# Log-softmax over 50000 columns: stores issued by SyncE between the loads, loads issued three tiles ahead

## The chip, the cores and the metric

The kernel runs on one core of a Trainium2 chip. The metric is the device time of one execution in microseconds. Before the change the median of three runs is 7614.17 us (7613.93 to 7614.27).

## The reference

For each of 16 x 512 = 8192 rows of 50000 float32 numbers, the log of the softmax:

```python
max_x = np.max(x, axis=-1, keepdims=True)
shifted = x - max_x
log_sum_exp = np.log(np.sum(np.exp(shifted), axis=-1, keepdims=True))
return (shifted - log_sum_exp).astype(np.float32)
```

1638.4 MB are read and as many written.

## The kernel before

The 8192 rows are cut into 512 tiles of 16 rows. Each row is cut into 8 pieces of 6250 numbers, and each piece lies on a partition of its own, so that a tile is 128 partitions x 6250 floats, 25000 bytes per partition, 3125 KB in all. A tile lives in one of 8 buffers (`NBUF`, pool `data`) from its load to its store; the result is written in place.

What is done with tile t stands in three helpers.

- `load(t)`: one DMA from the input to a buffer, issued by SyncE (line 75).
- `front(t)`: VectorE takes the maximum of each partition (`pmax`, line 81). Four small VectorE steps bring the 8 partial maxima of a row together and spread the negated row maximum over its 8 partitions (`allmax` L84, `rowmax` L86, `spread` L91, `negmax` L96). ScalarE takes the exponential of both halves with that bias, with the sum of each half into `part` (L102). TensorE adds the 16 partial sums of each row with a matrix of ones (L108), and ScalarE takes the logarithm (`logsum`, L112).
- `back(t)`: VectorE subtracts maximum and logarithm in place (L117). Then ScalarE issues the store (L121).

The order on each engine is the order of the program, since the scheduler is off (`manual_schedule`); only the semaphores are put in by the framework. The main loop sets that order:

```python
    for t in range(AHEAD):
        load(t)
    for t in range(ntiles + 1):
        if t < ntiles:
            front(t)
        if t >= 1:
            back(t - 1)
        if t + AHEAD < ntiles:
            load(t + AHEAD)
```

So VectorE takes the maximum of tile t before it ends tile t-1, and ScalarE issues the store of tile t-1 behind the exponentials of tile t. SyncE issues loads alone. `AHEAD` is 7. The load of tile t+7 takes the buffer that tile t-1 leaves, and waits until the store of tile t-1 has landed. The DMAs that SyncE issues go into queue 1 of the profile, those that ScalarE issues into queue 10. Both are served by the same 16 DMA engines: each engine gets 8 partitions of every transfer, that is 8 packets of 25000 bytes, and a packet of 4 bytes that counts the semaphore up.

Of the kernel before, what the change touches and what calls it, by code (L numbers as in the profile page):

```python
# [1 line left out]

# [4 lines left out]


FP32 = mybir.dt.float32
ACT = mybir.ActivationFunctionType  # L10
ALU = mybir.AluOpType
AX = mybir.AxisListType.X

P = 128
SQ = 32

G = 8
R = P // G
EXP_C = 3125
NBUF = 8  # L20
AHEAD = 7


@with_exitstack
def kernel(
    ctx: ExitStack,
    tc: tile.TileContext,
    x: bass.AP,
    out: bass.AP,
):  # L30
    nc = tc.nc
    xf = x.flatten_outer_dims()
    of = out.flatten_outer_dims()
    N, V = xf.shape
    W = V // G
    assert N % R == 0 and V % G == 0 and W % EXP_C == 0
    ntiles = N // R
    nexp = W // EXP_C

    xt = xf.rearrange("(t r) (g w) -> t (r g) w", r=R, g=G)  # L40
    ot = of.rearrange("(t r) (g w) -> t (r g) w", r=R, g=G)

    data = ctx.enter_context(tc.tile_pool(name="data", bufs=NBUF))
    stats = ctx.enter_context(tc.tile_pool(name="stats", bufs=4))
    consts = ctx.enter_context(tc.tile_pool(name="consts", bufs=1))
    dump_pool = ctx.enter_context(
        tc.tile_pool(name="dump", bufs=1, space=bass.MemoryType.PSUM)
    )
    sum_pool = ctx.enter_context(
        tc.tile_pool(name="sums", bufs=1, space=bass.MemoryType.PSUM)  # L50
    )

    ctx.enter_context(tc.manual_schedule())


    ones = consts.tile([P, P], FP32)
    nc.gpsimd.memset(ones, 1.0)  # L57
    ones3 = ones.rearrange("p (r g) -> p r g", g=G)
    nc.gpsimd.affine_select(  # L59
        out=ones3, in_=ones3, pattern=[[-G, R], [0, G]], base=0,  # L60
        channel_multiplier=1, compare_op=ALU.is_ge, fill=0.0,
    )
    nc.gpsimd.affine_select(  # L63
        out=ones3, in_=ones3, pattern=[[G, R], [0, G]], base=G - 1,
        channel_multiplier=-1, compare_op=ALU.is_ge, fill=0.0,
    )
    nc.scalar.preload_act_table_set("natural_log_exp_and_others")  # L67

    tiles = {}
    shift = {}  # L70
    logs = {}

    def load(t):
        buf = data.tile([P, W], FP32, name="buf")
        nc.sync.dma_start(out=buf, in_=xt[t])
        tiles[t] = buf

    def front(t):
        buf = tiles[t]
        pmax = stats.tile([P, 1], FP32, name="pmax")  # L80
        nc.vector.reduce_max(out=pmax, in_=buf, axis=AX)  # L81

        allmax = stats.tile([P, SQ], FP32, name="allmax")
        nc.vector.transpose(out=allmax, in_=pmax.to_broadcast([P, SQ]))  # L84
        rowmax = stats.tile([P, SQ // G], FP32, name="rowmax")
        nc.vector.tensor_reduce(  # L86
            out=rowmax, in_=allmax.rearrange("p (r g) -> p r g", g=G),
            op=ALU.max, axis=AX, negate=True,
        )
        spread = stats.tile([P, SQ], FP32, name="spread")  # L90
        nc.vector.tensor_copy(  # L91
            out=spread.rearrange("p (r g) -> p r g", g=G),
            in_=rowmax[:, :, None].to_broadcast([P, SQ // G, G]),
        )
        negmax = stats.tile([P, SQ], FP32, name="negmax")
        nc.vector.transpose(out=negmax, in_=spread)  # L96
        shift[t] = negmax

        part = stats.tile([P, nexp], FP32, name="part")
        for j in range(nexp):  # L100
            dump = dump_pool.tile([P, EXP_C], FP32, name="dump")
            nc.scalar.activation(  # L102
                out=dump, in_=buf[:, j * EXP_C : (j + 1) * EXP_C], func=ACT.Exp,
                bias=negmax[:, 0:1], scale=1.0, accum_out=part[:, j : j + 1],
            )
        rowsum = sum_pool.tile([P, 1], FP32, name="rowsum")
        for j in range(nexp):
            nc.tensor.matmul(  # L108
                rowsum, ones, part[:, j : j + 1], start=j == 0, stop=j == nexp - 1
            )  # L110
        logsum = stats.tile([P, 1], FP32, name="logsum")
        nc.scalar.activation(out=logsum, in_=rowsum, func=ACT.Ln)  # L112
        logs[t] = logsum

    def back(t):
        buf = tiles.pop(t)
        nc.vector.tensor_scalar(  # L117
            out=buf, in0=buf, scalar1=shift.pop(t)[:, 0:1], scalar2=logs.pop(t),
            op0=ALU.add, op1=ALU.subtract,
        )  # L120
        nc.scalar.dma_start(out=ot[t], in_=buf)  # L121

    for t in range(AHEAD):
        load(t)
# [9 lines that stand above are left out]
# [1 line left out]
_INS = ['x']  # L135
_OUTS = [((16, 512, 50000), 'float32')]


# [23 lines left out]
```

## Time and profile before

| | |
|---|---|
| median of three runs | 7614.17 us |
| profiled execution, its own time | 7614.27 us |
| its span | 7612.6 us |
| granted TensorE clock | 1.000 |
| VectorE busy | 5567.2 us, 73% |
| ScalarE busy | 3153.1 us, 41% |
| maximum L81, one instruction | 6664 ns |
| exponential L102, one instruction (two per tile) | 2869 ns |
| subtraction L117, one instruction | 3496 ns |
| idle time of VectorE before L81 | 1953.7 us |
| mean rate of the DMAs | 431 GB/s |

The span is the time from the first to the last instruction of the profiled execution; some 1.7 us of its time lie outside it. Busy shares are shares of the span. A group of instructions is named by line, engine, operation and tiles; behind it stand the busy time, the mean of one, the idle time of the engine just before the instructions of that group and what ended most of it. The DMA part of the page gives the packets, bytes and times by queue. Under that level the trace has a record of every packet, with queue, start, duration and bytes, but without the number of its engine.

### The profile page before, as it was taken

To read this page: it belongs to the slowest core of one execution; us is meant where nothing else is said; L and a number is where in the kernel's file an instruction comes from. 1 tells how busy PE (TensorE), PEld (TensorE's weight loads), DVE (VectorE), ACT (ScalarE), POOL (GpSimd) and SP (SyncE) were. 2 spreads that over 40 slices of the span, in tenths; PEclk is the share of its full clock that TensorE was granted. 3 is DMA by queue.
4 is the path that set the end of the run, shared out by engine and by line. 5 is a ranking of instruction groups with operands and counts; after the bars stand their busy time and mean duration, and the time that the engine had idled before them with its cause. 6 is when DMAs were issued, how large, how long until landed. Compare 5 with 4: busy or idle time off the path is not lost.

```text
span 7612.6 us, 12833 instructions
## 1 busy us (share of the span) xinstructions
PE 600.6 (8%) x2048; PEld 513.2 (7%) x2048; DVE 5567.2 (73%) x3072; ACT 3153.1 (41%) x2561; POOL 1.2 (0%) x7
## 2 busy tenths in 40 slices
PE   0000000000000000000000000000000000000000
PEld 0000000000000000000000000000000000000000
DVE  7777777777777777777777777777777777777776
ACT  4444444444444444444444444444444444444443
POOL 0000000000000000000000000000000000000000
DMA  9999999999999999999999999999999999999998
GB/s 425 433 432 432 432 432 432 432 432 432 432 432 432 432 432 432 432 432 432 432 432 432 432 432 432 432 432 432 432 432 432 432 432 432 431 432 432 432 432 380
DMA packets 147540, 3277.68 MB, mean 431 GB/s; under 512 B 16384, under 2 KB 16384, under 8 KB 16384
## 3 DMA queue, kind: packets, MB, share of 16 engines
q1 hardware_dynamic: 73728, 1638.43, 50.0%
q10 hardware_dynamic: 73728, 1638.43, 50.0%
q14 instruction: 68, 0.56, 0.0%
q8 instruction: 16, 0.26, 0.0%
HBM read 1638.40 MB, written 1638.40 MB: 430 GB/s over the span
## 4 chain that ended last, share of the span: by engine, by line
DVE 73%; another core or an unknown queue 25%; issue 1%; DMA 0%; ACT 0%; PE 0%; ACTq 0%
DVE pmax L81 45%; DVE buf L117 23%; DVE allmax L84 1%; DVE rowmax L86 1%; DVE spread L91 1%; DVE negmax L96 0%; DMA buf<-in_x_dram 0%; ACT dump L102 0%; PE rowsum L108 0%; ACT logsum L112 0%; ACTq L102 0%
## 5 line engine op out<-in xcount | busy, mean ns | idle before, releaser
L81 DVE TENSOR_REDUCE pmax<-buf 128x1 f32<-128x6250 f32 x512 | 3411.8, 6664 | 1953.7 <-DMA buf<-in_x_dram 1953.7
L102 ACT ACTIVATE dump<-buf,negmax 128x3125 f32<-128x3125 f32 x1024 | 2938.1, 2869 | 4092.9 <-DVE negmax L96 4029.5
L117 DVE TENSOR_SCALAR buf<-buf,negmax,logsum 128x6250 f32<-128x6250 f32 x512 | 1789.7, 3496 | 4.5 <-ACT logsum L112 3.6
L108 PE MATMUL rowsum<-part,ones 128*128 128x1 f32 x2048 | 600.6, 363 | 6991.7 <-ACT dump L102 6991.7
L108 PEld LDWEIGHTS rowsum<-part,ones 128*128 128x128 f32 x2048 | 513.2, 311 | 7079.0 <-ACT dump L102 7057.2
L112 ACT ACTIVATE logsum<-rowsum 128x1 f32<-128x1 f32 x512 | 87.6, 171 | 345.8 <-PE rowsum L108 345.8
L102 ACT ACTIVATION_READ_ACCUMULATOR dump<-buf,negmax 128x1 f32 x1024 | 191.1, 187 | 0.0
L96 DVE STREAM_TRANSPOSE negmax<-spread 128x32 f32<-128x32 f32 x512 | 108.2, 211 | 17.7
L84 DVE STREAM_TRANSPOSE allmax<-pmax 128x32 f32<-128x32 f32 x512 | 108.3, 211 | 17.4
L86 DVE TENSOR_REDUCE rowmax<-allmax 128x4 f32<-128x32 f32 x512 | 95.3, 186 | 17.7
L91 DVE COPY spread<-rowmax 128x32 f32<-128x32 f32 x512 | 92.9, 181 | 17.8
L67 ACT ACT_TABLE_LOAD x1 | 1.3, 1283 | 0.8 <-PEq L146 0.8
L59 POOL TENSOR_SCALAR_AFFINE_SELECT ones<-ones 128x128 f32<-128x128 f32 x1 | 0.4, 403 | 0.1
L63 POOL TENSOR_SCALAR_AFFINE_SELECT ones<-ones 128x128 f32<-128x128 f32 x1 | 0.4, 397 | 0.1
L57 POOL MEMSET ones<- 128x128 f32 x1 | 0.2, 204 | 0.3 <-POOLq L146 0.3
L146 POOL MEMSET const-bfloat16-1.0<- 128x1 bf16 x1 | 0.1, 101 | 0.0
L146 POOL MEMSET const-uint8-127<- 128x1 uint8 x1 | 0.1, 101 | 0.0
L146 POOL MEMSET const-float32-0.0<- 128x1 f32 x1 | 0.1, 98 | 0.3 <-issue 0.3
L146 POOL MEMSET const-float32-1.0<- 128x1 f32 x1 | 0.1, 98 | 0.0
## 6 DMA issues: line engine op xcount, KB each, us to landing
buf<-in_x_dram SPq DMA_DIRECT2D x512, 3125.0 KB, 51.9
out_dram<-buf ACTq DMA_DIRECT2D x512, 3125.0 KB, 37.5
```

The source lines that it names most:

```text
L59: nc.gpsimd.affine_select(out=ones3, in_=ones3, pattern=[[-G, R], [0, G]], base=0, channel_multiplier=1, compare_op=ALU.is_ge, fill=0.0,)
L63: nc.gpsimd.affine_select(out=ones3, in_=ones3, pattern=[[G, R], [0, G]], base=G - 1, channel_multiplier=-1, compare_op=ALU.is_ge, fill=0.0,)
L67: nc.scalar.preload_act_table_set("natural_log_exp_and_others")
L81: nc.vector.reduce_max(out=pmax, in_=buf, axis=AX)
L84: nc.vector.transpose(out=allmax, in_=pmax.to_broadcast([P, SQ]))
L86: nc.vector.tensor_reduce(out=rowmax, in_=allmax.rearrange("p (r g) -> p r g", g=G), op=ALU.max, axis=AX, negate=True,)
L91: nc.vector.tensor_copy(out=spread.rearrange("p (r g) -> p r g", g=G), in_=rowmax[:, :, None].to_broadcast([P, SQ // G, G]),)
L96: nc.vector.transpose(out=negmax, in_=spread)
L102: nc.scalar.activation(out=dump, in_=buf[:, j * EXP_C : (j + 1) * EXP_C], func=ACT.Exp, bias=negmax[:, 0:1], scale=1.0, accum_out=part[:, ...
L108: nc.tensor.matmul(rowsum, ones, part[:, j : j + 1], start=j == 0, stop=j == nexp - 1)
L112: nc.scalar.activation(out=logsum, in_=rowsum, func=ACT.Ln)
L117: nc.vector.tensor_scalar(out=buf, in0=buf, scalar1=shift.pop(t)[:, 0:1], scalar2=logs.pop(t), op0=ALU.add, op1=ALU.subtract,)
```

## The change

The store of a tile is issued by SyncE instead of ScalarE, and `AHEAD` is 3 instead of 7. Everything else stays, the 8 buffers and the main loop too. SyncE's order is then load 0, 1, 2, 3, store 0, load 4, store 1, load 5, and so on: store t-1, then load t+3. A store waits for L117 of its tile, and the load behind it in SyncE's order waits with it. All transfers go into the queue of SyncE.

```diff
 NBUF = 8
-AHEAD = 7
+AHEAD = 3
...
             op0=ALU.add, op1=ALU.subtract,
         )
-        nc.scalar.dma_start(out=ot[t], in_=buf)
+        nc.sync.dma_start(out=ot[t], in_=buf)
 
     for t in range(AHEAD):
         load(t)
```

## The prediction

> **What bounds the kernel now.** I read the page first (busy shares, slices, DMA queues), then the waits of VectorE and of SyncE's queue between 1000 and 7000 us, then the timeline of one tile, and last the DMA packets one by one.
>
> The page's engine line and its DMA lines:
>
> ```profile
> PE 600.6 (8%) x2048; PEld 513.2 (7%) x2048; DVE 5567.2 (73%) x3072; ACT 3153.1 (41%) x2561; POOL 1.2 (0%) x7
> ...
> DMA packets 147540, 3277.68 MB, mean 431 GB/s; under 512 B 16384, under 2 KB 16384, under 8 KB 16384
> ...
> q1 hardware_dynamic: 73728, 1638.43, 50.0%
> q10 hardware_dynamic: 73728, 1638.43, 50.0%
> ```
>
> No compute engine is over 73%. Queue 1 (loads, from SP) and queue 10 (stores, from ACT) fill 50.0% each of sixteen DMA engines' span: together the DMA engines have no free time. The waits in the steady stretch, VectorE's and SyncE's (us in total, times, longest):
>
> ```profile
> DVE pmax L81 <- DMA buf<-in_x_dram: 1556.5, 405, 4.6
> ```
>
> ```profile
> SPq L75 <- DMA out_dram<-buf: 5861.2, 405, 14.9
> ```
>
> VectorE waits for the load of every tile. SyncE stands 5861 of 6000 us before a load, waiting for the store that frees its buffer. One tile in the timeline (start, duration, what):
>
> ```profile
> 3016.73 6.66 DVE L81 TENSOR_REDUCE pmax<-buf 128x1 f32<-128x6250 f32 x1 [3.82 <-DMA buf<-in_x_dram]
> 3023.42 0.21 DVE L84 STREAM_TRANSPOSE allmax<-pmax 128x32 f32<-128x32 f32 x1
> ...
> 3024.24 3.49 DVE L117 TENSOR_SCALAR buf<-buf,negmax,logsum 128x6250 f32<-128x6250 f32 x1
> ...
> 3031.16 0.34 ACTq L121 DMA_DIRECT2D out_dram<-buf  x1
> 3031.58 6.66 DVE L81 TENSOR_REDUCE pmax<-buf 128x1 f32<-128x6250 f32 x1 [3.84 <-DMA buf<-in_x_dram]
> ```
>
> The period is 14.85 us and VectorE fills 11.0 of it (6.66 and 3.49 and four small steps). And the lead of the loads:
>
> ```profile
> buf<-in_x_dram SPq DMA_DIRECT2D x512, 3125.0 KB, 51.9
> out_dram<-buf ACTq DMA_DIRECT2D x512, 3125.0 KB, 37.5
> ```
>
> A load lands 51.9 us after its issue, 3.5 periods. The "seven ahead" of the code is 3.5 tiles in fact, because the buffer comes free so late.
>
> **The price of one transfer.** The packet records of the first four loads, which are alone in queue 1, give the last engine's landings at 10.68, 18.08, 25.49 and 32.89 us: 7.403 us each, with nothing between two transfers of one queue. So 1024 transfers need 1024 x 7.403 = 7580.7 us on each engine. The slowest engine has packets from 1.80 to 7611.25 us, 7609.4 us, and followed back from its last packet to the landing of the last load (7577.5 us) it has no gap. It is 28.7 us over 7580.7. These are packets that took over 928 ns (about 2% of all, most of them stores), and a share of the packets of kind "instruction" in the page's queue table (queue 8: 16 packets, 14.9 us; queue 14: 68 packets, 21.0 us), which land on a few engines. The load landings agree: VectorE's maxima from tile 32 to tile 480 are 14.857 us apart, 0.051 over 2 x 7.403, so 26 us in 512 tiles.
>
> A trap is the end. These windows of the DMA (last two columns: DMA share, GB/s) look as if 20 us could be won there:
>
> ```profile
> 4.00:32.00 28.00, 1.73 (x6) 1.50 (x6) 20.67 (x12) 11.91 (x8) 0.00 (x0) 1.00 1.00 430
> ...
> 1100.00:4100.00 3000.00, 236.44 (x806) 202.05 (x806) 2196.52 (x1212) 1242.92 (x1008) 0.00 (x0) 1.00 1.00 432
> ...
> 7560.00:7613.00 53.00, 2.93 (x10) 2.51 (x10) 25.28 (x13) 14.61 (x13) 0.00 (x0) 1.00 0.63 267
> ```
>
> The share falls to 0.63, but by the packets it is the thirteen engines ahead that idle. The one that ends last is full, so the idle of the others is worth nothing.
>
> **The change, part by part.** The sum is made against the profiled execution: 1.8 us to the first packet, 7609.4 of the slowest engine, 1.3 to the end of the span (7612.6 with rounding), and 1.7 outside it, 7614.3 in all, which is 0.1 over the median 7614.17.
>
> - *512 store issues leave ScalarE.* 0.338 us each, 173 us of a queue that idles 4029.5 us before L102 for VectorE. They lie beside that idle time: 0 us. Without that cover they would be worth at most these 173.
> - *512 store issues join SyncE.* SP then issues two transfers of about 0.33 us per 14.85 us: 0 us.
> - *The store's wait for L117 now stands ahead of a load.* From the landing of load t: 6.66 and 0.9 and 3.5 us of VectorE, then two issues, 0.7: store t-1 and load t+3 are out 11.8 us after that landing, and reach the engines up to 3.9 us later (the first store, issued at 32.91 into a busy engine, had its first packet at 36.76; into an idle engine it took 0.85). Queued on the slowest engine at the landing are store t-3, load t+1, store t-2 and load t+2: 4 x 7.4 = 29.6 us. Spare: 29.6 - 15.7 = 13.9 us. No gap on the slowest engine: 0 us. The faster engines may run out when they are more than 13.9 us ahead; they only wait for the slowest anyway.
> - *Load t+3 waits for the store of tile t-5*, queued ahead of load t-1, so landed long ago. The SP wait of 5861 us goes; late next is L117, for which SP will stand some 14 us per tile. Nothing is gained by its going, since the buffers were not what kept the DMA from working.
> - *The lead, seven to three.* As a loop: issue of store t-1 and load t+3 15.7 us after load t lands at worst, then 7.4 for the store and 7.4 for the load: 30.5 us for three tiles, 10.2 per tile, under 14.8. The DMA stays the longer one: 0 us.
> - *The start.* Loads 0 to 3 are issued at once and last until 32.9 us. L117 of tile 0 ended at 29.55, so store 0 and load 4 are out at 30.3, up to 3.9 us to the first packet: at most 1.3 us of gap, and I take 0, since 0.85 is the value of a ring that runs empty.
> - *The end.* After the last load the slowest engine still has stores 508, 509 and 510, 22.2 us. Store 511 is issued at most 18.9 us after the landing (7596.2 against 7577.5 now). No gap: 0 us.
> - *One ring instead of two.* The trace has no store followed by a load in one ring. Bounds: the four loads alone show 0 between transfers, the last four stores in queue 10 took 7.48 to 7.51 us on the slowest engine, 7.49 in the middle, where 7.403 is the price. If all stores cost that, 512 x 0.085 = 43.5 us are on the slowest engine in place of the 13.8 that are left of the 28.7 without queue 8's 14.9: +29.7. Below nothing: these 13.8 go, if alternation between two rings is what makes them. I take 0, by the nearest row, the loads in one ring with reads, and by the 928 ns that both kinds take in over 97% of the steady packets.
>
> Sum: 7614.3 + 0, so **7614 us**.
>
> A page of the Trainium skill speaks against one ring: "DMA: Bandwidth & Descriptors", in its section on the anatomy of one DMA (of the path that GpSimd issues), gives a fixed 2.0 us per DMA beside the bytes. Taken as a price in a queue it would make 1024 x 2.0 = 2048 us, an estimate by that page, and a time of some 9660. The four loads in one queue at 7.403 us apart leave no room for it: there it is latency of a landing, not time of the engine, and the sum goes by the row.
>
> **The rivals.**
> 1. *Stores in unbroken runs are dear.* Now each engine alternates load and store packets; in one ring eight store packets follow each other. For: the last four stores on the slowest engine took 7.49 us. Against: the other fifteen did the last store in 7.40, so that it is one engine's, and not one of runs as such. Price +29.7: 7644 us. It decides (over 0.2%, which is 15.2 us and about what a measurement of this kernel can tell from no change) from 0.03 us per store. Slower: 26%.
> 2. *The lead is too short.* If the order or a wait leaves one tile less, the loop is 30.5 us for two tiles, 15.2 each, 0.4 over the present 14.857: 512 x 0.4 = 205 us, 7820 us. For: SP now holds every load behind a wait on VectorE. Against: 13.9 us spare. 5%.
> 3. *Alternation is what costs now.* The 13.8 us go: 7600 us, which is within 0.2%; with half of the instruction packets out of the way too, 7593. For: most slow packets are stores in the mixed stretch. Against: mixed and alone, a packet takes 928 ns. 14%, of which 10% are under 7599.
> 4. *Nothing happens, since what is moved lay beside the DMA* (the forecast): 7614, with 7606 to 7622. 55%.
>
> **How the numbers follow.** The chance of a change within 0.2% (7599 to 7629) is rival 4 and the upper part of rival 3, 55 + 4 = 59%. Faster is the rest of rival 3, 10%, slower rivals 1 and 2, 31%. The range that holds 8 in 10 runs from 7598 (rival 3 nearly whole) to 7645 (rival 1 whole); it leaves out rival 2 and the far ends.
>
> **What would show each step.** Right: all packets in queue 1, near 100% of the engines; SP's wait on the store gone and one on L117 of some 14 us per tile in its place; time to landing 51.9 down to about 33 (3 x 14.85 - 11.8) for loads and 37.5 down to about 26 (five transfers less 11.8) for stores; VectorE's wait at L81 still some 3.8 us per tile; the period 14.85. Rival 1 would show in a longer store on all engines, a period over 14.89. Rival 2 shows as slices with a DMA share under 0.98 and a longer wait at L81. Rival 3 shows as a period near 14.82. The prediction is wrong if the DMA share stays at 1.00 and packets take another time than 928 ns, or if the share falls in the middle.

## The result and the profile after

The changed kernel takes 7740.82 us (median of 4 runs, 7735.56 to 7747.93), 1.0166 times the kernel before (95% interval 1.0149 to 1.0184): slower by 1.7%. The range on record ended at 7645. The profiled execution took 7735.9 us, with a span of 7734.2.

The page after, rates in 40 slices and the queue of all transfers:

```profile
GB/s 417 426 425 430 429 431 431 431 431 430 431 431 431 431 431 431 431 431 431 431 431 429 431 429 424 419 417 418 418 415 420 417 417 413 416 417 416 416 419 381
...
q1 hardware_dynamic: 147456, 3276.87, 100.1%
```

The DMA engines are full from end to end, as before, in one queue. But the rate is not one number: it starts low, stands at 431 from the sixth slice, and sinks from the 24th slice on, near 4500 us, to some 417. Before it stood at 431 to 433 in all slices but the first and the last. Two stretches of each kernel, before first (the last two columns are DMA share and GB/s):

```profile
1100.00:4100.00 3000.00, 236.44 (x806) 202.05 (x806) 2196.52 (x1212) 1242.92 (x1008) 0.00 (x0) 1.00 1.00 432
4900.00:7100.00 2200.00, 174.07 (x594) 148.70 (x594) 1609.51 (x889) 912.82 (x741) 0.00 (x0) 1.00 1.00 432
```

```profile
1100.00:4100.00 3000.00, 235.78 (x805) 201.37 (x805) 2189.99 (x1207) 1237.52 (x1006) 0.00 (x0) 1.00 1.00 431
4900.00:7100.00 2200.00, 167.68 (x572) 143.25 (x572) 1557.11 (x859) 882.42 (x716) 0.00 (x0) 1.00 1.00 417
```

The share is 1.00 in both stretches: the DMA engines do not wait for work, the packets themselves are longer. The waits of SyncE and of VectorE between 1000 and 7000 us, and the DMA issues, are as foretold:

```profile
SPq L121 <- DVE buf L117: 5635.7, 398, 15.1
```

```profile
DVE pmax L81 <- DMA buf<-in_x_dram: 1621.6, 399, 5.0
```

```profile
buf<-in_x_dram SPq DMA_DIRECT2D x512, 3125.0 KB, 33.4
out_dram<-buf SPq DMA_DIRECT2D x512, 3125.0 KB, 26.5
```

SP stands 14.2 us per tile before a store, a load lands 33.4 us after its issue and a store 26.5. So the order on SP does what the code says, and VectorE waits for loads as before, only longer late in the run.

**Where the 121.6 us between the two profiled executions came from.** From the start of each tile's maximum (L81) in the two traces, after minus before: 15.1 us at tile 64, 25.6 at tile 288, 125.4 at tile 511; the end gives 3.8 back. That is three stretches: 15.1 us in the first 64 tiles, 0.047 us per tile in the next 224, and 0.45 us per tile in the last 223. The 3.8 are no price: with a shorter lead a load comes later among the stores, so that less is left to store behind the last one. By that, some 11 us of the 15.1 are lost in the first tiles.

Two things in the records of landings go with it. Each transfer lands 16 times, once per DMA engine. *Spread* is the time between the first and the last of the 16; *in step* is the largest number of engines whose landings of one load fall within 1 us. Medians over 32 tiles (spread: 64), with the period from one load's last landing to the next:

| changed kernel, tiles | spread, us | engines in step | period, us |
|---|---|---|---|
| 0 to 31 | 3.4 | 8 | (start) |
| 64 to 95 | 8.2 | 4 | 14.91 |
| 192 to 223 | 14.8 | 4 | 14.90 |
| 256 to 287 | 16.6 | 4 | 14.92 |
| 288 to 319 | 16.6 | 6 | 14.95 |
| 320 to 351 | 18.2 | 10 | 15.33 |
| 448 to 479 | 18.0 | 13 | 15.38 |

The spread grows until it stands at 18 us, the engines that are ahead gather, and the period jumps. The long packets lie at the change of direction. In the first store of the run the eight packets take 928 ns each but for the last two, 976 and 1308; in the load behind it the first two take some 1030 and 1000. Late in the run (5000 to 7000 us), one of the two kinds of transfer has a last packet of some 1230 ns in the mean; from 2000 to 4000 us it is 936. The engine that lands last sets the time, and it is the last to run out of work; still its packets are long too. Followed back from its landings between 5000 and 7000 us, the packets of its load make 7.81 us in the mean and those of its store 7.59, where eight of 928 ns make 7.42. The longest is the seventh of the load, 1.17 us, which is not at the engine's own change of direction.

So the experiments start from **theory A**: in one ring (the queue of one issuing engine) every DMA engine turns from a store to a load and back, and the turn costs up to half a microsecond when most engines make it at the same moment; a short lead holds the engines that are ahead and lines them up. **Rival B**: the lead is too short and engines run dry. **Rival C**: stores in one ring are dear by themselves, as rival 1 of the prediction had it.

### The profile page after: what moved, and what is told of

Its sections match the earlier page's. It is cut to its first block, busy times and chain, and to the rows that moved or that the text cites. A ratio compares the mean times of both kernels' runs of the same rounds, so it can differ in the third digit from the quotient of the medians.

```text
span 7734.2 us, 12836 instructions
## 1 busy us (share of the span) xinstructions
PE 600.3 (8%) x2048; PEld 512.9 (7%) x2048; DVE 5567.3 (72%) x3072; ACT 3153.1 (41%) x2561; POOL 1.2 (0%) x7
## 4 chain that ended last, share of the span: by engine, by line
DMA 74%; DVE 24%; SPq 1%; issue 1%; ACT 0%; PE 0%; ACTq 0%
DMA buf<-in_x_dram 74%; DVE pmax L81 15%; DVE buf L117 8%; SPq L121 1%; DVE allmax L84 1%; DVE rowmax L86 0%; DVE spread L91 0%; DVE negmax L96 0%; ACT dump L102 0%; SPq L75 0%; PE rowsum L108 0%; ACT logsum L112 0%; ACTq L102 0%
## 5 line engine op out<-in xcount | busy, mean ns | idle before, releaser
L81 DVE TENSOR_REDUCE pmax<-buf 128x1 f32<-128x6250 f32 x512 | 3411.7, 6663 | 2078.9 <-DMA buf<-in_x_dram 2078.9
L117 DVE TENSOR_SCALAR buf<-buf,negmax,logsum 128x6250 f32<-128x6250 f32 x512 | 1789.8, 3496 | 4.5 <-ACT logsum L112 3.6
## 6 DMA issues: line engine op xcount, KB each, us to landing
buf<-in_x_dram SPq DMA_DIRECT2D x512, 3125.0 KB, 33.4
out_dram<-buf SPq DMA_DIRECT2D x512, 3125.0 KB, 26.5
```

The lines of the kernel that those rows point to most:

```text
L117: nc.vector.tensor_scalar(out=buf, in0=buf, scalar1=shift.pop(t)[:, 0:1], scalar2=logs.pop(t), op0=ALU.add, op1=ALU.subtract,)
```

## The experiments

**The lead alone.** Stores stay on ScalarE:

```diff
-AHEAD = 7
+AHEAD = 3
```

> The lead of three tiles alone: stores stay on ScalarE's queue. Theory A (in one ring, the step from a store to a load costs up to 0.5 us when most DMA engines make it at the same moment; a short lead brings the engines into step): with two rings every engine alternates packet by packet and there is no such step, so 7614 us within 10, whatever the lead. Rival B (the lead of three is too short, the DMA engines run dry): as slow as the changed kernel, 7700 to 7760 us. Rival C (stores in one ring are dear as such, whatever the lead): 7614 us too.

Measured: 7613.96 us, ratio 1.0000 (0.9991 to 1.0009). The loads still land 51.9 us after their issue:

```profile
buf<-in_x_dram SPq DMA_DIRECT2D x512, 3125.0 KB, 51.9
out_dram<-buf ACTq DMA_DIRECT2D x512, 3125.0 KB, 37.5
```

That is less of a test than I had thought. With the stores elsewhere, SyncE's list holds loads and nothing to wait for but buffers, so it is the eight buffers that set the lead, not `AHEAD`. It shows that the number alone does nothing; it does not speak on B.

**One ring with other leads.** The changed kernel, with

```diff
-AHEAD = 3
+AHEAD = 4
```

and 6, 7, 2 and 5.

> One ring with a lead of four tiles instead of three. In the changed kernel the spread between the first and the last engine's landing of one transfer grows by some 3.3 us in 1000 us until it stands at 17.7 us from about 4400 us on, and there the period goes from 14.90 to 15.35 us. Theory A: one tile more lets the spread grow to some 32 us before the engines ahead are held and fall into step; at 3.3 us in 1000 us that is not reached in the run. The period stays at 14.90 to the end and the time is 7635 to 7655 us. Rival B: 7614 to 7640 us, with fewer long packets from the start. Rival C: no change, 7735 to 7750 us.

> One ring with a lead of six tiles. With 8 buffers the load of tile t+6 waits for the store of tile t-2 on all engines, and behind that store an engine has only a load and a store left (14.8 us less the time of a landing and an issue): the engines ahead are held at some 11 to 13 us. Theory A: they fall into step sooner than with three tiles, from about 2400 us on, so 7760 to 7830 us, slower than with three although the loads are issued further ahead. Rival B: not slower than with three, 7614 to 7740 us. Rival C: 7740 us.

> The moved store alone, with the lead of seven as before. The load of tile t+7 waits for the landing of the store of tile t-1, which is the last transfer in the ring, and the next store is issued behind that load. All theories expect that the DMA engines run dry once per tile for the time from a landing to the next first packet, some 2 to 2.5 us: a period of 16.8 to 17.3 us, 8600 to 8860 us, and a DMA share of 0.85 to 0.88. Theory A adds the price of the step in step, up to 0.5 us a tile: up to 9100 us.

> One ring with a lead of two tiles. A load and a store are queued behind the landing that lets the next pair go, 14.8 us, and the pair comes 11.8 to 15.7 us after it: the engines ahead are held at a spread of 0 to 3 us from the first tile on. Theory A: the price of engines in step, 0.4 us and more a tile, is paid by all 512 tiles, and some of the ring runs dry: 7850 to 8200 us, over one ring with six tiles. Rival C: 7740 us.

> One ring with a lead of five tiles. The load of tile t+5 waits for the landing of the store of tile t-3, behind which four transfers are left, 29.6 us, less some 1.4 us (with six tiles two transfers are left, 14.8 us, and the spread stood at 13.4): the engines ahead are held at some 28 us. In the run with four tiles the spread passed 28 us near 6000 us. Theory A: the period is 14.90 us up to about 6000 us and 15.4 to 15.8 after it, 7680 to 7735 us: slower than with four tiles, faster than with three. If the lead by itself were what counts, it would be no slower than with four: 7644 us.

| AHEAD | us | ratio to before (interval) | spread stands at | engines in step, tiles 448 to 479 | period there |
|---|---|---|---|---|---|
| 2 | 7905.31 | 1.0382 (1.0363 to 1.0401) | 2.8 from the start | 14 | 15.47 |
| 3 (the change) | 7740.82 | 1.0166 (1.0149 to 1.0184) | 18 from tile 300 | 13 | 15.38 |
| 4 | 7644.0 | 1.0039 (1.0025 to 1.0053) | still growing, 31 | 3 | 14.91 |
| 5 | 7664.96 | 1.0076 (1.0059 to 1.0093) | 26.7 from tile 400 | 7 | 14.91 |
| 6 | 7902.95 | 1.0382 (1.0366 to 1.0397) | 11.8 from tile 140, 13.4 from tile 210 | 8 | 15.77 |
| 7 | 9713.06 (one run) | | 0.9 throughout | | 19.1 |

With four tiles the sink in the second stretch is gone (one ring with four, then with six tiles):

```profile
4900.00:7100.00 2200.00, 173.59 (x592) 148.33 (x592) 1603.66 (x884) 909.93 (x740) 0.00 (x0) 1.00 1.00 431
```

```profile
1100.00:2400.00 1300.00, 102.62 (x350) 87.68 (x350) 946.38 (x523) 538.72 (x437) 0.00 (x0) 1.00 1.00 431
4900.00:7100.00 2200.00, 163.62 (x558) 139.79 (x558) 1522.33 (x840) 859.76 (x698) 0.00 (x0) 1.00 1.00 407
```

Six tiles run at 431 until the spread comes to its limit and then at 407, although the loads are asked for earlier. The reader should see why a longer lead is worse here: with 8 buffers, the load of tile t+6 waits for the store of tile t-2, and SP waits on another thing than with three:

```profile
SPq L75 <- DMA out_dram<-buf: 5638.4, 388, 15.6
```

Behind that store each engine has two transfers left, so an engine can be no more than about 14.8 us ahead. With three tiles it is what is queued behind a landing (29.6 us) less the 11.8 us that VectorE and the issues take and the 0.85 of a first packet: 17.0, measured 18. Theory A named the size for four tiles (7635 to 7655, measured 7644.0) and the order of three, four and six; it named six too low (7760 to 7830). B had six no slower than three. C falls here: the stores are the same in all of them, and it had three, four and six alike.

Seven tiles, the moved store alone, has a gap of 2.3 us per tile on each engine by the packet records:

```profile
1100.00:4100.00 3000.00, 185.29 (x632) 158.28 (x632) 1714.63 (x945) 972.55 (x790) 0.00 (x0) 1.00 0.88 337
```

I expected 8600 to 8860 from that gap, up to 9100 with the price of the turn. The gap is as expected. The other 1.9 us per tile are long packets: all 16 engines are within 0.9 us, the first packet of the load, which comes right after the gap, takes 1.60 us and its last two 1.45 and 1.59; those of the store behind it take 928 ns. In step, right after a gap, the price is four times what I had put.

Five tiles missed its forecast (7680 to 7735). The spread came to its limit as computed (26.7, expected 28, near 5900 us), but in the profiled execution, at 7642.49 the fastest of four (the others 7658.79 to 7685.6), only seven engines gathered and the period stayed at 14.91. So being held is not itself the price. That it gathers the engines fits the table; that it gathered more of them in the three longer executions is not shown, since they have no trace.

Nor does the number in step give the size of the price: seven engines paid nothing here, with six tiles eight paid 0.87 us per tile over 14.90, with two tiles fourteen paid 0.57. How much of the price of a held ring comes from being in step, and how much from a ring that has only just been filled again, these runs do not separate.

**Twice the turns.** Every transfer is cut into two halves of the columns, in the order store, store, load, load ("grouped"), or store, load, store, load ("alternate"). The heart of the second edit, where `st` is the tile to be stored:

```diff
-        nc.sync.dma_start(out=buf, in_=xt[t])
...
+        for h in range(2):
+            c = slice(h * EXP_C, (h + 1) * EXP_C)
+            if st is not None:
+                nc.sync.dma_start(out=ot[st[0]][:, c], in_=st[1][:, c])
+            if buf is not None:
+                nc.sync.dma_start(out=buf[:, c], in_=xt[t][:, c])
```

> The changed kernel with every transfer cut into two halves of 3125 columns, in the order store, store, load, load: twice the transfers, as many steps from store to load as before. Theory A (the price lies in the step from one direction to the other when the engines are in step): as the changed kernel, 7720 to 7780 us. Rival C (the stores are dear by themselves, or each transfer is): 7740 if by bytes, over 7800 if by transfer.

> The same halves in the order store, load, store, load: four changes of direction per tile instead of two, the same bytes, the same transfers, the same lead. Theory A: the price of the changes is paid twice, 7820 to 7950 us, 60 us at least over the grouped halves. Rivals B and C: as the grouped halves, within 30 us.

Measured: grouped 7867.69 us, ratio 1.0328 (1.0310 to 1.0347); alternate 8034.86, 1.0557 (1.0541 to 1.0573). The second stretch, grouped and then alternate:

```profile
4900.00:7100.00 2200.00, 166.65 (x568) 142.37 (x568) 1539.46 (x847) 873.53 (x710) 0.00 (x0) 1.00 1.00 412
```

```profile
4900.00:7100.00 2200.00, 160.80 (x548) 137.39 (x548) 1492.85 (x823) 843.19 (x686) 0.00 (x0) 1.00 1.01 399
```

Grouped is over its forecast for two reasons: twice the transfers cost 0.2 us a tile where nobody is held (15.10 against 14.90), and the limit of the spread comes at tile 192 instead of 300. By its number alone it would also fit C with a price by transfer. Between the two the turns decide: C had them within 30 us of each other, and they are 167 apart, though the alternate order too is over the range that A had named. Both have a period of 15.10 us at tiles 64 to 127; from tile 256 on it is 15.48 to 15.61 (means of 32 tiles) with two turns and 16.02 to 16.08 with four. So 0.45 us for two turns and 0.96 for four, with the same bytes, transfers and lead.

**The transfers alone.** All arithmetic is left out; SP's order is that of the changed kernel, or the stores go to ScalarE's ring:

> All arithmetic is left out: the input is loaded and stored as it is, in one ring, in the order of the changed kernel (store t-1, load t+3). No engine waits for VectorE, six transfers are queued behind a landing, and almost no instructions are fetched, so that nothing brings the DMA engines out of step. Theory A: engines in step pay at the change of direction from the first to the last tile, as in the first 30 tiles of the changed kernel (15.03 us a tile) or more: 7690 to 7900 us. Rival B (only an engine that runs dry pays): 512 x 14.81 us, 7580 to 7600 us.

> The same copy with the stores in ScalarE's ring and a lead of seven, arithmetic left out. Theories A, B and C: no step in one ring, 512 x 14.81 us, 7580 to 7600 us; the difference to the kernel before, some 20 us, is what instruction fetches and slow packets cost there.

Measured: 7634.86 us in one ring, 7602.67 in two. The forecast of A for one ring was wrong in size (7690 to 7900), that of B too low (7580 to 7600), and two rings came out just over theirs (7580 to 7600). The windows show why A was wrong, first one ring, then two (the last two columns are DMA share and GB/s):

```profile
40.00:240.00 200.00, 0.00 (x0) 1.00 1.00 420
...
1100.00:4100.00 3000.00, 0.00 (x0) 1.00 1.00 431
```

```profile
40.00:240.00 200.00, 0.00 (x0) 1.00 1.00 432
...
1100.00:4100.00 3000.00, 0.00 (x0) 1.00 1.00 432
```

The first 15 tiles in one ring have a period of 15.1 to 15.3 us, while the spread goes from 0.8 to 2.4. Then the spread passes 3.6 us, the period falls to 14.82 to 14.87 and stays under 14.90 to the end. Two rings hold a spread of 0.7 us over the same tiles at 14.81. So the engines come apart while they pay, and then they stop paying; in the changed kernel the short lead stops them from drifting further. Six transfers are queued behind every landing in this copy, so no engine was dry in those first tiles: B cannot explain them.

**Held engines in two rings.** The kernel before with fewer buffers:

```diff
-NBUF = 8
-AHEAD = 7
+NBUF = 6
+AHEAD = 5
```

> The kernel before (two rings) with 6 buffers instead of 8 and AHEAD 5. In two rings SyncE's order holds loads alone, so that it is the buffers that set the lead, and the run with AHEAD 3 and 8 buffers left it at 8. With 6 the engines ahead are held where the spread reaches some 10 to 15 us, as in one ring with three or six tiles. Theory A: being held, or in step, costs nothing where the packets of loads and stores alternate: 7610 to 7630 us. Rival B (an engine that is held or runs dry pays, in any ring): 7700 us and more.

Measured: 7616.19 us, ratio 1.0002 (0.9993 to 1.0012). A load lands 22.3 us after its issue instead of 51.9, the spread stays at 4.3 to 9.4 us, and 9 to 12 engines are in step at a period of 14.86. So this lead is shorter than that of the changed kernel, nearly as many of its engines are in step, and where load and store packets alternate it costs 2 us, which is not clear of nothing. One of its ten executions took 7730.48 us, the others 7615.7 to 7618.4, and the ratio is that of the nine; the one has no trace, so what it spent the time on is open.

```profile
buf<-in_x_dram SPq DMA_DIRECT2D x512, 3125.0 KB, 22.3
out_dram<-buf ACTq DMA_DIRECT2D x512, 3125.0 KB, 37.5
...
4900.00:7100.00 2200.00, 174.04 (x594) 148.75 (x594) 1609.91 (x889) 911.69 (x743) 0.00 (x0) 1.00 1.00 431
```

That ends B in the form that an engine that is held or runs dry pays in any ring.

**A faster one?** TensorE's instructions halved, in the kernel before:

```diff
-        for j in range(nexp):
-            nc.tensor.matmul(
-                rowsum, ones, part[:, j : j + 1], start=j == 0, stop=j == nexp - 1
-            )
+        both = stats.tile([P, 1], FP32, name="both")
+        nc.scalar.activation(
+            out=both, in_=part[:, 0:1], func=ACT.Identity, bias=part[:, 1:2], scale=1.0,
+        )
+        nc.tensor.matmul(rowsum, ones, both, start=True, stop=True)
```

> The kernel before with the two partial sums added by ScalarE and one matmul per tile instead of two (the same result). It halves TensorE's instructions and with them the 16 packets of queue 8 (14.9 us in all) that share one DMA engine. If that engine is the one that ends last: 7 us less, 7606 to 7608 us. If not: 7614 us.

Measured: 7614.44 us, ratio 1.0000 (0.9991 to 1.0009), with 8 packets in queue 8 instead of 16:

```profile
q8 instruction: 8, 0.13, 0.0%
```

So those packets do not set the end. No run with the whole computation beat the kernel before by more than its interval. The copy in two rings, 11 us under it, shows what the same transfers take in this order without the computation.

## Why the prediction was wrong, point by point

- *The DMA engines are the bound, by packets, and the idle of the engines ahead is worth nothing.* Right: the share is 1.00 before and after, and with 6 buffers, where the end of the run has less idle, the time is the same.
- *The store issues cost nothing on either queue; SP's wait moves to L117 at some 14 us a tile; landings 33 and 26 us after the issue.* Right: 14.2, 33.4 and 26.5.
- *"The faster engines may run out when they are more than 13.9 us ahead; they only wait for the slowest anyway."* This step failed. They do reach the limit (18 us, since a first packet on a ring that runs low takes 0.85 us and not 3.9), but there they gather, and from then on packets are longer on all engines, the slowest too: 7.81 and 7.59 us for its load and store, where the sum had 7.403. Measured 0.45 us per tile over the last 223 tiles, 100 of the 121.6 us.
- *"One ring instead of two ... I take 0."* This failed as well, in size. The bounds were 0 and +29.7. With a lead of four tiles, where no engines gather, one ring costs 30.0 us (7644.0 against 7614.0), and in the copies 32.2 (7634.86 against 7602.67). These come close to the upper bound, but by luck: the bound stands for slow stores on one engine, and the 14.9 us that it takes off for queue 8 are not on the path, since half of those packets could go and the time stayed. Had they been left in, the bound would be +14.8. With four tiles the maxima (L81) fall behind those of the kernel before by 3.7 us up to tile 64 and by 0.049 us per tile from there on, which the sum had at nothing. The nearest row that I chose, four loads in one ring, holds no turn; and I had no row for a turn in step, which is what the rest of the price is. The range ended at that bound because I had put the turn and the lead into separate cases: neither alone gives 7741.
- *Rival 1, unbroken store runs.* Its sum, 7644, is the time of one ring with four tiles, but its mechanism is not shown: out of step all packets are some 3 ns longer (931 against 928), not the stores alone. Its test, a period over 14.89, did come (14.90, then 15.35).
- *Rival 2, the lead too short.* The lead does matter, but not as a loop that runs dry: the share stays at 1.00 until the last tiles, and a still shorter lead in two rings costs nothing that is clear of noise.
- *Rival 3, alternation costs.* The other way round: alternation is what makes the turn free.
- *The start and the end at 0.* The start was not: some 11 us are lost in 64 tiles, in which the engines begin in step (median spread 3.4 us). The 3.8 us that come back at the end are order, not speed.

On the use of several issuers, the Trainium skill, "DMA: Bandwidth & Descriptors", in its rules for kernel authors, says that spreading DMAs over SP, ACT and GpSimd brings no bandwidth and only saves issue time. Here the same transfers took 7602.67 us from two issuers and 7634.86 from one, with an issue of 0.33 us that lies under 14.8: the measurement decides, and it says that two rings are worth 0.4% here, where loads and stores are mixed, and more where the lead is short. The same page, in its section on queues, rings and completion order, says that an engine goes round the rings for which it has work, packet by packet, and that a packet typically holds some 9 to 17 descriptors. The records before agree as to going round: on an engine the starts alternate between queue 1 and queue 10, 925 ns apart, after every record of 25000 bytes. Whether such a record is what the page calls a packet, no run here shows.

What stays open: why the turn is dear when many engines make it together, why its price does not follow their number, and why the slowest engine pays inside a transfer and not at its own turn. The records give durations of packets, not what a packet waits for; whether it is the memory, a port or the read of the next transfer was not tried. Also open is why the executions with five tiles differ by up to 43 us, and which engine ends last.

## What to carry to other kernels

Where loads and stores fill the DMA engines, give them two issuing engines, so that each DMA engine has a packet of the other kind at hand; in this kernel a single ring costs 0.4% even at its best. A share of 1.00 does not say that the rate is the same: compare GB/s by stretch, and look at how far the 16 engines are apart. If one ring it must be, find the lead at which the engines ahead are held last: with 8 buffers it was four tiles, and the medians with fewer and with more were slower.

## What the runs showed of the hardware

- Sixteen DMA engines that all turn from one direction to the other within 1 to 3 us pay 0.4 to 0.6 us per tile for it (two turns: the first tiles of the copy, and one ring with two tiles); when the copy had them 4 us and more apart, some 0.05. Gathered at the limit of a larger spread they paid 0.45 (three tiles) and 0.87 (six). Right after a gap it was 1.9.
- While they pay, they come apart: from 0.8 to 3.6 us in some 20 tiles of the copy, where two rings held 0.7. Left alone, the price ended itself; a lead that ran out renewed it.
- Where nothing holds them, the engines drift apart: by 3 to 4 us in 1000 us, up to 32 us at the end of the kernel before (median of the last 32 tiles), and 26 in the two-ring copy, which has hardly any instructions to fetch (16 packets in queue 14).
